# Modulation units over whole k, low one-hot rows on VectorE, chunk loads three ahead, and one gathered prompt row with each batch of the gate table

## The chip, the cores and the metric

The kernel runs on one core of a Trainium2 chip. The metric is the device time of one execution in microseconds. The profile names the engines PE (TensorE matmuls), PEld (its weight loads), DVE (VectorE), ACT (ScalarE), POOL (GpSimd) and SP (SyncE, which here only issues DMA transfers). L997 is line 997 of the kernel before.

## The reference

The kernel computes one inference step of two post-norm layers for 128 prompt tokens and 256 latent tokens of width 1024. Cut to what matters here:

```python
def adaln(cond, w, b):
    m = jax.nn.silu(cond) @ w + b                  # w: 1024 x 6144 in each layer, two vectors cond
    return jnp.split(m[..., None, :], 6, axis=-1)  # shift, scale, gate, twice

def layer(x, l, cond, ctx):
    sh1, sc1, g1, sh2, sc2, g2 = adaln(cond, w_mod[l], b_mod[l])
    y, new_ctx = token_mixer(modulate(x, sh1, sc1), ...)     # projections, three mixers, output product
    x = layer_norm(DN_ALPHA * x + g1 * y, ...)
    f = peer(modulate(x, sh2, sc2), ...)
    return layer_norm(DN_ALPHA * x + g2 * f, ...), new_ctx

def peer(h, wq, keys, u_tab, v_tab):               # 16384 experts, 8 heads x 16 of them for each token
    ...                                            # e: chosen experts, g: their gates
    act = jax.nn.gelu(einsum('td,ted->te', tb, u_tab[eb])) * gb
    return einsum('te,ted->td', act, v_tab[eb])
```

## The kernel before

The stages follow one another in each layer: start or norm, mixer (projections, three branches, output product), routes (queries and the choice of experts), gate table, expert loop, tail.

All weights arrive as tiles of 128 x 1024 f32 (512 KB) in a pool `wst`, tag `w`, with 8 buffers. SP issues these loads in order; a load waits until a buffer is free, and what stands behind it on SP waits too. Projections run block by block: `blocks` loads a block of `w_in`, `split` casts it on ScalarE (`uh`, L222) and subtracts on VectorE or GpSimd (`ul`, L224), and `proj3` multiplies (L368 to L370).

A modulation unit (`adaln_unit`) yields some columns of `w_mod` for both conditioning vectors. It runs 32-row matmuls in four quadrants of the PSUM tile (L259), copies the sum (L261, `modp`), and the next unit's call finishes it. Before, a unit is 256 columns: two loads, eight matmuls with k spread over the quadrants, two selection products (L265) which add the quadrants, and two ScalarE steps with the bias (L268). There are 48 units: 8 at the start, 16 and 8 as fill between the blocks of the two mixers, 4 in each layer ahead of the routes (the rest of the list in layer 1), 10 during the routes of layer 0. A matmul of f32 by f32 shows as two records in the trace.

Prompt tokens take their experts' rows by gather: GpSimd fetches a 128 x 1024 tile of rows (`prow`, L1057 for u, L1068 for v; 256 in a layer), VectorE multiplies and sums it (L1062 or L1073). `slots` decides how many lie behind which instruction.

Latent tokens go through all 128 chunks of 128 experts. `u_load` fetches a chunk of `peer_uT`, `u_product` multiplies it (L1164 for the first 35 chunks in f32, L1167 to L1169 afterwards in three parts). The first 35 products run during routes and gate table. `gate_table` builds for 16 tokens at a time (16 batches in a layer) the dense table of gates: VectorE makes one-hot rows `oa`, `ol` (L997, L999) and `oh` (L1001), ScalarE scales the low rows `ol` token by token (L1004), TensorE multiplies (L1014, L1015, 32 matmuls in a batch), ScalarE copies out (L1018), and SP writes two 512 KB pieces to `gd` in DRAM. With each batch go W_RATE gathered rows. The expert loop then takes for each chunk the u product, the gates `gt` back from `gd` (L1219, 512 KB in four chunks), and the v product (L1243 to L1245); the remaining rows are spread over its chunks at the pace of

```python
w = (c + 2) * 10 - (10 - P_TAIL) * max(0, c + 2 - (128 - LAG))
slots(n_win + -(-(256 - n_win) * w // (10 * (128 - P_END) - (10 - P_TAIL) * (LAG - P_END))), last[0])
```

where n_win is the number of rows done by the end of the gate table, and P_TAIL, P_END and LAG are 5, 6 and 36: 10/1070 of the rows with each chunk, and half of it in the tail, where only v products are left.

Tile pools and a scheduler set the order of the instructions on each engine.

Of the kernel before, what the change touches and what calls it, by code (L numbers as in the profile page):

```python
# [155 lines left out]
def hybrid_step(ctx: ExitStack, tc: tile.TileContext, A, O):  # L156
# [71 lines left out]
    fill_ps, fill_n, first = [None], [0], [0]  # L228


    def cond_prep(sp, ps1):
# [12 lines left out]
        for l in range(DEPTH):
            bm = mk(sp, [48, 128], "bm", bufs=2)
            dma(out=bm, in_=A["b_mod"][l].rearrange("(k p) -> k p", p=128))
            ps = mk(ps1, [128, 512], "pt")
            T.transpose(ps[:, :48], bm, ident[:48, :48])
            V.tensor_copy(bmT[:, l], ps[:, :48])
            for part in (1, 4):  # L250
                V.tensor_scalar(bmT[:, l, part * KD:(part + 1) * KD], bmT[:, l, part * KD:(part + 1) * KD], 1.0, None, op0=ALU.add)
# [1107 lines left out]
```

## Time and profile before

| | us |
|---|---|
| median of three timed runs | 2998.48 |
| lowest and highest | 2995.82, 3007.12 |
| the profiled execution's own time | 3004.09 |
| its span, first to last instruction | 3002.3 |
| TensorE, VectorE, ScalarE, GpSimd busy | 2855.6, 2309.1, 1396.8, 824.8 |
| DMA | 767.09 MB, 256 GB/s over the span |

Busy time is the union of an engine's instructions; TensorE's matmuls overlap and their ends are modelled, so a busy TensorE is not one at its peak. The rows of a later section are read as follows. A row of a table by stretch has the stretch, its length, then for each engine the busy time and the instructions, the granted TensorE clock (1.00 is 2.4 GHz), the DMA's busy share and GB/s. A row of the timeline has start, duration, engine, line, operation, output and inputs, how many were merged, and in brackets the idle time before it with its releaser.

### The profile page before, as it was taken

The numbers are of one execution on the slowest core, as the hardware profiler recorded it, in microseconds if no ns is written. First come the engines' busy times: TensorE is split into PE (matmuls) and PEld (weight loads), VectorE is DVE, ScalarE is ACT, GpSimd is POOL, SyncE is SP. The second block draws the span as 40 slices with busy tenths as digits, with TensorE's granted clock in tenths as the row PEclk, the third lists the DMA queues.
The fourth block names the chain that finished last, engine by engine and source line by source line (L and its number), as shares of the span: only waits on it lengthen the run. The fifth ranks groups of instructions, "written<-read, shape, count | busy, mean of one in ns | idle before, by whom it ended". The sixth has DMA issues, their size and how long they took to land.

```text
span 3002.3 us, 48719 instructions
## 1 busy us (share of the span) xinstructions
PE 2855.6 (95%) x17953; PEld 2479.3 (83%) x17953; DVE 2309.1 (77%) x4888; ACT 1396.8 (47%) x2861; POOL 824.8 (27%) x566
## 2 busy tenths in 40 slices
PE   7999999999889999999969999999987999999996
PEld 5888889877779999998858888898876999999985
DVE  3645654599669999998976466547986999999988
ACT  4544543225754444444445455432178544444443
POOL 1000000002334455554540000000033444555554
PEclk9999999999889999999979999999999999999998
DMA  6454322565999999999934432233569999999994
GB/s 246 151 159 146 95 72 87 182 223 167 316 364 408 391 392 396 393 391 369 379 97 144 127 93 74 85 111 113 156 217 371 418 395 392 394 391 394 393 364 166
DMA packets 299328, 767.09 MB, mean 256 GB/s; under 512 B 42770, under 2 KB 113874, under 8 KB 299090
## 3 DMA queue, kind: packets, MB, share of 16 engines
q1 hardware_dynamic: 225362, 495.51, 46.2%
q0 software_dynamic: 73728, 268.47, 23.5%
q8 instruction: 141, 2.31, 0.3%
q14 instruction: 97, 0.79, 0.1%
HBM read 726.92 MB, written 36.96 MB: 254 GB/s over the span
## 4 chain that ended last, share of the span: by engine, by line
PE 74%; DVE 11%; DMA 6%; ACT 4%; issue 4%; POOL 1%; SPq 0%; POOLq 0%; ACTq 0%; DVEq 0%
PE hp L1167 6%; PE out L1243 6%; PE hp L1169 6%; PE out L1245 6%; PE hp L1168 6%; PE out L1244 6%; PE pp L368 5%; PE pp L369 5%; PE pp L370 5%; PE hp L1164 4%; DMA w<-in_peer_uT 3%; PE pp L947 2%; ACT ol L1004 2%; DVE vl L224 2%; DVE tn L1073 2%
## 5 line engine op out<-in xcount | busy, mean ns | idle before, releaser
L1057 POOL DMA_INDIRECT prow<-in_peer_u,ei x256 | 363.1, 1418 | 763.1 <-DVE prow L1062 523.5
L1068 POOL DMA_INDIRECT prow<-in_peer_v,ei x256 | 382.4, 1494 | 350.1 <-DVE tn L1073 308.6
L222 ACT CAST vh<-w 128x1024 fp32r<-128x1024 f32 x256 | 268.9, 1050 | 367.9 <-issue 285.8
L1167 PE MATMUL hp<-hh,uh 128*128 128x256 f32 x1488 | 434.7, 292 | 0.0
L1169 PE MATMUL hp<-hh,ul 128*128 128x256 f32 x1488 | 417.1, 280 | 0.0
L1168 PE MATMUL hp<-hl,uh 128*128 128x256 f32 x1488 | 416.5, 280 | 0.0
L1245 PE MATMUL out<-vh,al 128*128 128x512 f32 x1024 | 400.0, 393 | 3.6 <-DVE al L1230 3.6
L1244 PE MATMUL out<-vl,ah 128*128 128x512 f32 x1024 | 397.5, 390 | 2.9 <-DVE vl L224 2.9
L1243 PE MATMUL out<-vh,ah 128*128 128x512 f32 x1024 | 392.9, 400 | 1.4 <-ACT ah L1228 1.4
L224 DVE TENSOR_TENSOR vl<-w,vh 128x1024 fp32r<-128x1024 f32 x256 | 315.8, 1234 | 62.7 <-ACT vh L222 44.0
L1073 DVE SCALAR_TENSOR_TENSOR tn<-prow,pact,tn 128x1024 f32<-128x1024 f32 x254 | 325.4, 1281 | 2.7
L1155 ACT CAST uh<-w 128x1024 fp32r<-128x1024 f32 x186 | 195.2, 1050 | 252.6 <-PE hp L1168 240.6
L368 PE MATMUL pp<-hh,uh 128*128 128x384 f32 (+1 forms) x848 | 297.9, 351 | 7.5 <-ACT hh L344 3.8
L1062 DVE SCALAR_TENSOR_TENSOR prow<-prow,tn 128x1024 f32<-128x1024 f32 x256 | 302.4, 1219 | 0.1
L1164 PE MATMUL hp<-hs,w 128*128 128x256 f32 x1120 | 270.1, 398 | 30.0 <-DMA w<-in_peer_uT 30.0
L370 PE MATMUL pp<-hh,ul 128*128 128x384 f32 (+1 forms) x848 | 297.0, 350 | 1.4 <-POOL ul L224 1.4
L369 PE MATMUL pp<-hl,uh 128*128 128x384 f32 (+1 forms) x848 | 294.8, 348 | 0.2 <-DVE xr L494 0.2
L1167 PEld LDWEIGHTS hp<-hh,uh 128*128 128x128 f32 x1488 | 281.1, 189 | 0.0
L1169 PEld LDWEIGHTS hp<-hh,ul 128*128 128x128 f32 x1488 | 281.1, 189 | 0.0
L1168 PEld LDWEIGHTS hp<-hl,uh 128*128 128x128 f32 x1488 | 281.1, 189 | 0.0
L224 DVE TENSOR_TENSOR ul<-w,uh 128x1024 fp32r<-128x1024 f32 x124 | 149.8, 1208 | 162.2 <-ACT uh L222 158.2
L1164 PEld LDWEIGHTS hp<-hs,w 128*128 128x128 f32 x1120 | 218.8, 200 | 63.4 <-DMA w<-in_peer_uT 33.1
(401 smaller groups left out, 5637.9 us busy)
## 6 DMA issues: line engine op xcount, KB each, us to landing
w<-in_peer_uT SPq DMA_DIRECT2D x256, 512.0 KB
w<-in_peer_v SPq DMA_DIRECT2D x256, 512.0 KB
w<-in_w_in SPq DMA_DIRECT2D x104, 512.0 KB
w<-in_w_mod SPq DMA_DIRECT2D x96, 512.0 KB
gd<-w SPq DMA_DIRECT2D x64, 512.0 KB
gt<-gd SPq DMA_DIRECT2D x64, 512.0 KB
w<-in_peer_wq SPq DMA_DIRECT2D x32, 512.0 KB
w<-in_w_branch SPq DMA_DIRECT2D x24, 512.0 KB
```

The lines of the kernel that those rows point to most:

```text
L224: e.tensor_tensor(lo, src, hi.bitcast(F32), op=ALU.subtract)
L368: T.matmul(o, wh[:, k, :], hh[:, k, :], start=(k == 0), stop=False)
L369: T.matmul(o, wh[:, k, :], hl[:, k, :], start=False, stop=False)
L370: T.matmul(o, wl[:, k, :], hh[:, k, :], start=False, stop=(k == KD - 1))
L1073: V.scalar_tensor_tensor(acc, row, act[:, j:j + 1], acc, op0=ALU.mult, op1=ALU.add)
L1164: T.matmul(o, ut[0][:, k, :], hs[:, k, :], start=(k == 0), stop=(k == KD - 1))
L1167: T.matmul(o, uh[:, k, :], hh[:, k, :], start=(k == 0), stop=False)
L1168: T.matmul(o, uh[:, k, :], hl[:, k, :], start=False, stop=False)
L1169: T.matmul(o, ul[:, k, :], hh[:, k, :], start=False, stop=(k == KD - 1))
L1243: T.matmul(o, ah[:, ts], vh[:, ns], start=f, stop=False)
L1244: T.matmul(o, ah[:, ts], vl[:, ns], start=False, stop=False)
L1245: T.matmul(o, al[:, ts], vh[:, ns], start=False, stop=e)
```

## The change

Five things are done. A modulation unit now takes 1024 columns over all eight k: eight loads, 32 matmuls in which each quadrant holds other columns, two transposes in place of the selection products, and additions with the bias on VectorE; there are 12 units (2 at the start, 5 and 2 slots for fill after every sixth block, 1 ahead of the routes, 3 at blocks 9, 12 and 15 of the routes). The conditioning vectors and the bias arrive already transposed. The low one-hot rows are multiplied by one VectorE instruction per batch, with glT in f16. The first three chunks of peer_uT are loaded ahead of the loop and each step loads the chunk three further on. W_RATE is 1 instead of 2.

```diff
-W_RATE = 2
+W_RATE = 1
-N_FILL = (16, 8)
-N_AD = (4, 4)
+N_FILL = (5, 2)
+FILL_BY = 6
+N_AD = (1, 1)
+U_AHEAD = 3
-R_AD = 4
+UNITS = [((0, 0, 0, 4), (0, 1, 0, 4)), ((0, 0, 4, 4), (0, 1, 4, 4))]
+UNITS += [((l, part, 0, 8),) for l, part in ((0, 2), (0, 3), (0, 4), (1, 0), (1, 1), (0, 5), (1, 2), (1, 3), (1, 4), (1, 5))]
...
     def cond_prep(sp, ps1):
-        cond = mk(sp, [16, 128], "cond")
-        dma(out=cond[0:8, :], in_=A["c_ctx"].rearrange("(k p) -> k p", p=128))
-        dma(out=cond[8:16, :], in_=A["c"].rearrange("o (k p) -> (o k) p", p=128))
+        cond = mk(sp, [128, 16], "cond")
+        dma(out=cond, in_=A["cond"])
+        dma(out=bmT, in_=A["b_mod"])
...
-    def adaln_unit(l, part, hb, ps1, tags):
-
-        w = load_k(A["w_mod"][l, part * 4 + hb])
+    def adaln_unit(u, ps1, tags):
+
         ps = mk(ps1, [128, 512], tags[0])
         for k in range(KD):
-            q = k % 4
-            T.matmul(ps[32 * q:32 * q + 32, :256], condT[:, k, :], w[k], start=(k < 4), stop=(k >= 4), tile_position=(0, 32 * q))
+            w = mk(wst, [128, RAWC], "w")
+            dma(out=w, in_=A["w_mod"][u, k])
+            for q in range(4):
+                T.matmul(ps[32 * q:32 * q + 32, :256], condT[:, k, :], w[:, q * 256:(q + 1) * 256], start=(k == 0), stop=(k == KD - 1), tile_position=(0, 32 * q))
         mp = mk(outer, [128, 256], "modp", bufs=2)
         S.copy(mp, ps[:, :256])
         yield
         pt = mk(ps1, [128, 512], tags[1])
         for a in range(2):
-            T.matmul(pt[:, 2 * a:2 * a + 2], mp[:, a * 128:(a + 1) * 128], sel, start=True, stop=True)
-        c = part * KD + 2 * hb
-        for a in range(2):
-            S.activation(mcol[:, l, part, 2 * hb + a, :], pt[:, 2 * a:2 * a + 2], AF.Identity, bias=bmT[:, l, c + a:c + a + 1])
+            T.transpose(pt[:, a * 128:(a + 1) * 128], mp[:, a * 128:(a + 1) * 128], ident)
+
+        pv = pt[:, :256].rearrange("p (a q m) -> p q a m", a=2, q=4)
+        j = 0
+        for l, part, k0, n in UNITS[u]:
+            for c in range(2):
+                V.tensor_tensor(mcol[:, l, part, k0:k0 + n, c].rearrange("p (q a) -> p q a", a=2), pv[:, j // 2:(j + n) // 2, :, c],
+                                bmT[:, l, part * KD + k0:part * KD + k0 + n].rearrange("p (q a) -> p q a", a=2), op=ALU.add)
+            j += n
...
             yield load_w(src[b0 + j])
-            if j % 2 and fill_n[0] > 0:
+            fill_at[0] += 1
+            if fill_n[0] > 0 and fill_at[0] % FILL_BY == 0:
                 fill_n[0] -= 1
                 adaln(1, fill_ps[0], ("pp", "pt"))
...
                 for k in range(KD):
-                    if k % 2 == 0:
-                        adaln(2, ps1, ("pp", "pt"), True)
+                    if k % 4 == 0:
+                        adaln(1, ps1, ("pp", "pt"), True)
...
-        glT = mk(rp, [128, NS], "glT")
+        glT = mk(rp, [128, NS], "glT", dt=F16)
...
-                slot(V.tensor_tensor(oh, ol, bc(ghT), op=ALU.mult))
-                for r in range(TB):
-                    o = ol[:, r // 2, :, r % 2]
-                    S.activation(o, o, AF.Copy, scale=glT[:, b * TB + r:b * TB + r + 1])
+                V.tensor_tensor(oh, ol, bc(ghT), op=ALU.mult)
+                slot(V.tensor_tensor(ol, ol, bc(glT), op=ALU.mult))
...
-        u_load(0)
+        for c in range(U_AHEAD):
+            u_load(c)
 
         def u_step(i):
-            if i + 1 < LAG - 1:
-                u_load(i + 1)
+            if i + U_AHEAD < LAG - 1:
+                u_load(i + U_AHEAD)
             u_product(i)
...
-            if l == 0 and b >= N_WQ + R_AD:
+            if l == 0 and b in (9, 12, 15):
                 adaln(1, pu, ("uT", "hp"), b == 15)
```

On VectorE, in the gate table of layer 0, two batches before stand like this (oa, ol and ohh are one-hot rows, prow a gathered row with its sum hd):

```order
L997 TENSOR_TENSOR oa_7010<-iot_6854,i1T_6850 128x2048
L999 TENSOR_TENSOR ol_7012<-iot_6854,i2T_6851 128x2048
L1001 TENSOR_TENSOR ohh_7014<-ol_7012,ghT_6852 128x2048
L1062 SCALAR_TENSOR_TENSOR prow_7016,hd_6888<-prow_7016,tn_4726 128x1024
L1062 SCALAR_TENSOR_TENSOR prow_7019,hd_6888<-prow_7019,tn_4726 128x1024
L997 TENSOR_TENSOR oa_7095<-iot_6854,i1T_6850 128x2048
```

and at the same place of the change like this:

```order
L1001 TENSOR_TENSOR ol_6893<-iot_6704,i2T_6701 128x2048
L1003 TENSOR_TENSOR ohh_6895<-ol_6893,ghT_6702 128x2048
L999 TENSOR_TENSOR oa_6971<-iot_6704,i1T_6700 128x2048
L1004 TENSOR_TENSOR ol_6893<-ol_6893,glT_6703 128x2048
L1062 SCALAR_TENSOR_TENSOR prow_6898,hd_6739<-prow_6898,tn_4628 128x1024
L1001 TENSOR_TENSOR ol_6973<-iot_6704,i2T_6701 128x2048
```

A batch has five VectorE instructions in both; the multiply by glT has taken the place of one row, and the next batch's oa stands ahead of it.

On SP, in the mixer of layer 0, the loads before alternate between two blocks of w_in and the two tiles of a unit:

```order
L210 DMA w_1050<-in_w_mod 128x1024
L210 DMA w_1052<-in_w_mod 128x1024
L210 DMA w_1480<-in_w_in 128x1024
L210 DMA w_1512<-in_w_in 128x1024
L210 DMA w_1544<-in_w_mod 128x1024
```

and at the same place of the change (the last two blocks ahead of a unit, the unit, the next block):

```order
L214 DMA w_1378<-in_w_in 128x1024
L214 DMA w_1410<-in_w_in 128x1024
L255 DMA w_1443<-in_w_mod 128x1024
L255 DMA w_1449<-in_w_mod 128x1024
L255 DMA w_1455<-in_w_mod 128x1024
L255 DMA w_1461<-in_w_mod 128x1024
L255 DMA w_1467<-in_w_mod 128x1024
L255 DMA w_1473<-in_w_mod 128x1024
L567 DMA out_new_state_ssd<-so_814 128x4x64
L255 DMA w_1479<-in_w_mod 128x1024
L255 DMA w_1485<-in_w_mod 128x1024
L567 DMA out_new_state_ssd<-so_824 128x4x64
```

The next block's load (w_1498) now follows behind these eight.

## Rows read from the trace of the kernel before

**Rows 1.** The page, the chain that ended last, by engine.
```profile
PE 74%; DVE 11%; DMA 6%; ACT 4%; issue 4%; POOL 1%; SPq 0%; POOLq 0%; ACTq 0%; DVEq 0%
```

**Rows 2.** Table by stretch: engines' busy us, granted clock, DMA share, GB/s.
```profile
50.00:525.00 475.00, 468.65 (x2951) 402.22 (x2950) 264.47 (x577) 216.28 (x501) 10.96 (x6) 0.98 0.38 121
717.00:862.00 145.00, 118.67 (x855) 100.69 (x853) 93.01 (x114) 113.59 (x344) 53.03 (x32) 0.90 0.92 301
...
868.00:900.00 32.00, 32.00 (x201) 29.24 (x201) 30.83 (x48) 17.00 (x25) 15.78 (x11) 0.94 1.03 418
...
1142.00:1400.00 258.00, 258.00 (x1690) 233.28 (x1689) 246.96 (x271) 119.86 (x177) 131.77 (x94) 1.00 1.01 393
1411.00:1500.00 89.00, 88.34 (x422) 71.94 (x422) 86.20 (x115) 43.38 (x60) 45.65 (x25) 1.00 0.98 368
...
2196.00:2321.00 125.00, 100.34 (x787) 85.30 (x785) 92.80 (x114) 111.08 (x339) 50.20 (x32) 0.95 0.98 333
2250.00:2275.00 25.00, 20.75 (x155) 17.91 (x156) 20.12 (x24) 23.65 (x75) 10.25 (x7) 0.93 1.08 375
```

**Rows 3.** Chain of the gate-table stages, by line, and two of its pieces.
```profile
by line: DMA w<-in_peer_uT 31.4%; PE hp L1164 28.6%; ACT ol L1004 17.1%; ACT w L1018 6.0%; DMA gd<-w 3.9%; DMA gt<-gd 3.0%; issue 2.6%; PE pn L1015 1.1%; PE pn L1014 0.9%; DVE ohh L1001 0.8%; PE pp L1014 0.8%; PE pp L1015 0.8%; DVE oa L997 
by line: DMA w<-in_peer_uT 28.9%; ACT ol L1004 27.8%; PE hp L1164 14.8%; ACT w L1018 10.5%; DMA gd<-w 4.8%; DMA gt<-gd 3.2%; issue 3.2%; SPq L1021 1.6%; DVE ohh L1001 0.9%; ACT gel L1171 0.9%; DVE oa L997 0.9%; DVE ol L999 0.9%; PE pn L1015
...
746.21 10.01 DMA w<-in_peer_uT
...
760.73 3.52 PE hp L1164 x16
```

**Rows 4.** Line L997 in each layer (first and last start), and its neighbours' timeline.
```profile
L997 DVE TENSOR_TENSOR oa<-iot,i1T x16: 1218/1221/1226, 716.6 to 843.4; 128x2048 f16<-128x2048 f16 x16
L997 DVE TENSOR_TENSOR oa<-iot,i1T x16: 1218/1225/1226, 2194.8 to 2299.6; 128x2048 f16<-128x2048 f16 x16
...
734.31 1.22 DVE L997 TENSOR_TENSOR oa<-iot,i1T 128x2048 f16<-128x2048 f16 x1
769.86 0.22 PE L1014 MATMUL pn<-ohh,oa 128*128 128x128 f16 x1 [0.28 <-ACT w L1018]
771.41 4.82 ACT L1004 ACTIVATE ol<-ol,glT 128x128 f16<-128x128 f16 x16
771.76 3.67 PE L1164 MATMUL hp<-hs,w 128*128 128x256 f32 x16
```

**Rows 5.** Groups by line: busy us, mean ns of one, idle before.
```profile
L1001 DVE TENSOR_TENSOR ohh<-ol,ghT 128x2048 f16<-128x2048 f16 x32 | 39.2, 1224 | 1.0
L1073 DVE SCALAR_TENSOR_TENSOR tn<-prow,pact,tn 128x1024 f32<-128x1024 f32 x254 | 325.4, 1281 | 2.7
L222 ACT CAST uh<-w 128x1024 fp32r<-128x1024 f32 (+1 forms) x130 | 134.6, 1038 | 203.8 <-PE pp L369 162.2 <-issue 24.0 <-PE pb L691 12.4
L224 DVE TENSOR_TENSOR ul<-w,uh 128x1024 fp32r<-128x1024 f32 x124 | 149.8, 1208 | 162.2 <-ACT uh L222 158.2 <-PE pt L412 2.8 <-PE pt L265 0.5
```

**Rows 6.** The start: timeline, a piece of the chain, GB/s from 4 to 50 us.
```profile
4.13 24.35 SPq L210 DMA_DIRECT2D w<-in_w_mod  x16
21.84 1.26 ACT L444 ACTIVATE hraw<-pa,mcol 128x128 f32<-128x128 f32 x3
24.00 0.51 ACT L344 CAST hh<-hraw 128x384 fp32r<-128x384 f32 x1
51.78 0.69 PE L370 MATMUL pp<-hh,ul 128*128 128x384 f32 x1 [1.44 <-POOL ul L224]
...
9.71 3.85 DMA w<-in_w_mod
...
GB/s 394 346 413 389 395 413 417 420 374 417 420 413 424 424 410 417 342 232 256 239 214 196 367 324 256 264 228 214 128 388 356 175 319 24 0 0 6 6 156 381
```

**Rows 7.** Chain during the routes: pieces of one modulation unit.
```profile
599.13 0.56 PE uT L259 x6
599.69 0.54 PE hp L265 x4
```

More of the change, by code (lines that the diff above doesn't have):

```diff
@@ L227, in hybrid_step @@
     spool = [None]
-    fill_ps, fill_n, first = [None], [0], [0]
+    fill_ps, fill_n, fill_at, first = [None], [0], [0], [0]
     def cond_prep(sp, ps1):
-        cond = mk(sp, [16, 128], "cond")
-        dma(out=cond[0:8, :], in_=A["c_ctx"].rearrange("(k p) -> k p", p=128))
-        dma(out=cond[8:16, :], in_=A["c"].rearrange("o (k p) -> (o k) p", p=128))
+        cond = mk(sp, [128, 16], "cond")
+        dma(out=cond, in_=A["cond"])
+        dma(out=bmT, in_=A["b_mod"])
         V.memset(condT, 0.0)
-        ps = mk(ps1, [128, 512], "pt")
-        T.transpose(ps[:, :16], cond, ident[:16, :16])
@@ L238, in cond_prep @@
         th = mk(sp, [128, 16], "cth")
-        S.activation(th, ps[:, :16], AF.Tanh, scale=0.5)
+        S.activation(th, cond, AF.Tanh, scale=0.5)
         cc = mk(sp, [128, 16], "cc")
-        S.activation(cc, ps[:, :16], AF.Copy, scale=0.5)
+        S.activation(cc, cond, AF.Copy, scale=0.5)
         V.scalar_tensor_tensor(condT[:, :, 0:2].rearrange("p k c -> p c k"), th.rearrange("p (c k) -> p c k", c=2), 1.0,
                                cc.rearrange("p (c k) -> p c k", c=2), op0=ALU.add, op1=ALU.mult)
[L244 to L251, printed above, removed]
@@ L253, in adaln_unit @@
-    def adaln_unit(l, part, hb, ps1, tags):
-        w = load_k(A["w_mod"][l, part * 4 + hb])
+        for part in (1, 4):
+            b = bmT[:, :, part * KD:(part + 1) * KD]
+            V.tensor_scalar(b, b, 1.0, None, op0=ALU.add)
+    def adaln_unit(u, ps1, tags):
         ps = mk(ps1, [128, 512], tags[0])
         for k in range(KD):
-            q = k % 4
-            T.matmul(ps[32 * q:32 * q + 32, :256], condT[:, k, :], w[k], start=(k < 4), stop=(k >= 4), tile_position=(0, 32 * q))
+            w = mk(wst, [128, RAWC], "w")
+            dma(out=w, in_=A["w_mod"][u, k])
+            for q in range(4):
+                T.matmul(ps[32 * q:32 * q + 32, :256], condT[:, k, :], w[:, q * 256:(q + 1) * 256], start=(k == 0), stop=(k == KD - 1), tile_position=(0, 32 * q))
@@ L264, in adaln_unit @@
         for a in range(2):
-            T.matmul(pt[:, 2 * a:2 * a + 2], mp[:, a * 128:(a + 1) * 128], sel, start=True, stop=True)
-        c = part * KD + 2 * hb
-        for a in range(2):
-            S.activation(mcol[:, l, part, 2 * hb + a, :], pt[:, 2 * a:2 * a + 2], AF.Identity, bias=bmT[:, l, c + a:c + a + 1])
-    todo = []
-    for l, ps in ((0, (0, 1)), (0, (2,)), (0, (3, 4)), (1, (0, 1)), (0, (5,)), (1, (2,)), (1, (3, 4)), (1, (5,))):
-        todo += [(l, part, hb) for hb in range(4) for part in ps]
+            T.transpose(pt[:, a * 128:(a + 1) * 128], mp[:, a * 128:(a + 1) * 128], ident)
[6 more added lines that the diff above has]
+            j += n
+    todo = list(range(len(UNITS)))
     begun = []
@@ L277, in adaln @@
         for _ in range(min(n, len(todo))):
-            u = adaln_unit(*todo.pop(0), ps1, tags)
+            u = adaln_unit(todo.pop(0), ps1, tags)
             next(u)
@@ L449, in mixer @@
                 ln_mod_T(l, t, 0, 1, sp, mk(sp, [128, D], "xn", bufs=3), ps1, "pt", raw, lambda ks: parts(raw[:, ks], hh[:, ks, ts], hl[:, ks, ts], V if t == 2 else G))
-        fill_ps[0], fill_n[0], first[0] = ps1, N_FILL[l], N_FIRST
+        fill_ps[0], fill_n[0], fill_at[0], first[0] = ps1, N_FILL[l], 0, N_FIRST
         ysT = [mk(mo, [128, 4, NTOK], f"y{i}", dt=F32 if i else F32R) for i in range(3)]
@@ L1329, in blocked @@
     d["peer_wq"] = cut(d["peer_wq"], KD, 128)[:, :, 0]
-    d["w_mod"] = cut(d["w_mod"], 4, 256)
+    m = d["w_mod"].reshape(DEPTH, KD, 128, 6, KD, 128)
+    d["w_mod"] = np.stack([np.concatenate([m[l, :, :, part, k0:k0 + n].reshape(KD, 128, n * 128) for l, part, k0, n in u], axis=2) for u in UNITS])
+    d["b_mod"] = d["b_mod"].reshape(DEPTH, 48, 128).transpose(2, 0, 1)
+    d["cond"] = np.concatenate([d.pop("c_ctx").reshape(KD, 128), d.pop("c").reshape(KD, 128)]).T
     d["w_out"] = cut(d["w_out"], 4, 256)
```

## Prediction

> **What bounds the kernel now.** I read the page first: TensorE holds 74% of the chain that ended last, VectorE 11% and the DMA 6% [rows 1]. One core, so no other core's time matters. Then the table of busy time by stretch [rows 2], because the average hides three different regimes in each of the two layers. In the long expert loop (row 1142 to 1400) TensorE is busy in all of it, VectorE in 246.96 of 258 us (96%) and the DMA moves 393 GB/s. In the loop's tail (1411 to 1500) VectorE is busy 86.20 of 89 us. In the gate-table stage (717 to 862 and 2196 to 2321) nobody is full: TensorE 118.67 of 145 us at a granted clock of 0.90, VectorE 93.01, ScalarE 113.59.
>
> Third, the chain by line in the gate-table stage [rows 3]: the wait for a chunk of `peer_uT` is 31.4% of it in layer 0 and 28.9% in layer 1, ScalarE's `ol` at L1004 17.1% and 27.8%. One such wait is 10.01 us, for a product (16 L1164 matmuls) that takes 3.52 us. So this is a stage of late loads, and I look for the gain there.
>
> **The change, part by part.** The sum is made on the profiled execution's own 3004.1 us; the median of the three timed runs, 2998.5 us, lies 5.6 us below it, and I move the result down by that.
>
> *Gate table, 16 batches a layer.* The 16 ScalarE instructions a batch (4.82 us together, [rows 4]) go; one VectorE multiply of the form of L1001 (1224 ns) comes [rows 5]; one row's product goes from the batch. VectorE so has five operations a batch as before. Unhindered, its first three batches took from 716.6 to 734.31 us, 5.9 us each [rows 4]; that stays its floor. Over all 15 intervals the batches took (843.4-716.6)/15 = 8.45 us in layer 0 and (2299.6-2194.8)/15 = 6.99 in layer 1 [rows 4]. TensorE's floor in layer 0: 21 chunk products over 16 batches, 1.31 x 3.52 us, and 1.9 us for the batch's 32 f16 matmuls (from the first at 769.86 to the next product at 771.76, [rows 4]), 6.5 us; in layer 1 17 products, 1.06 x 3.52 + 1.9 = 5.6 us. DMA: a batch writes 1.05 MB of table, gathers one row of 0.52 MB instead of two, and loads 0.69 or 0.56 MB of chunks: 2.26 and 2.13 MB, at 375 GB/s (best row of this stage, 2250 to 2275 [rows 2]) 6.0 and 5.7 us. The chunks are asked for three products early, some 10 us ahead at 3.5 us each, about the 10.01 us of the longest kind of wait. The likely periods are a little above the highest floor, 6.7 and 6.2 us: 15 x 1.75 = 26 and 15 x 0.8 = 12 us. Behind the last batch those 4.82 us become one VectorE step of 1.2: 3.6 us a layer. Together **-45 us**. Bounds: -60 at the floors; -12 if the chunks come as late as now and only the ScalarE part helps.
>
> *The 16 rows a layer that leave the batches* go to the expert loop: 240 instead of 224 rows, at the pacing of L1274 (224 x 10/1070) 2.24 a chunk instead of 2.09. A chunk has 38 TensorE records, so 1690 records in 258 us are 5.80 us a chunk [rows 2]. VectorE gets 0.15 x 1.28 us (L1073, [rows 5]) = 0.19 us more, 3.3% of the chunk: 96% becomes 99%. It stays just under TensorE, which hides it; if that cover is gone the excess is paid, so I take +3 us for both layers, 0 to 10. DMA: 1.05 MB of u and v, 0.13 of the table, 2.24 x 0.524 of rows: 2.36 MB in 5.80 us, 406 GB/s. The row 868 to 900 shows 418 GB/s with TensorE full, so I take this as hidden. The tail has no such cover: 30 of the rows' products lie there and become 32; two at 1.28 us a layer, **+5 us**.
>
> *Start.* Sixteen `w_mod` loads are issued from 4.13 on [rows 6], before and after. Before, 8 units run in four rounds of load, product, copy, selection, columns; the first block's products stall for `ul` until 51.78. Now two rounds. At about 400 GB/s (first entries of the GB/s row) 8.4 MB behind 2.2 MB of constants and x have landed by some 28 us; copy, transposes and adds are 2 us; the ScalarE steps for two k run from 21.84 to 24.51, 1.33 us each, so four k are 5.3 us and with two casts between them 7.4. First full product near 38 to 40: **-12 us**, range -6 to -14.
>
> *Units elsewhere.* Products and bytes are equal: one new unit is four old. The four selection matmuls of an old unit (0.54 us [rows 7]) become two transposes in a new one: 40 old units outside the start become 10, so at least 30 x 0.54 = 16 us of TensorE leave, nearly all in stretches where it is the chain; I take **-15**. The additions move to VectorE, 28 small ones, under its other work.
>
> *Eight loads in one burst.* This is where the change adds a wait. The pool `w` has 8 buffers and SP issues in order, so the next block's load stands behind the unit's eight and gets a buffer only when TensorE has done the unit's first k. Behind it wait the cast, the subtraction, and TensorE's next product. A load in a quiet stretch took 3.85 us [rows 6], cast and subtraction 1.04 and 1.21 [rows 5]: 6.1 us. Meanwhile TensorE has the rest of the unit: 64 matmuls at 0.56/6 us [rows 7] are 6.0 us, less the first k 5.2. So about 1 us a unit, ten units: **+10 us**, from 0 to 74 (a landing of 10.01 us gives 12.3-4.9 = 7.4 each). By DMA: Bandwidth & Descriptors of the Trainium skill (section Anatomy of one DMA), a transfer costs about 2 us fixed plus its bytes at 436 GB/s, by estimate 3.2 us for such a load; by that the stall would be 0.4 us a unit and the sum 6 us lower. That section was measured on another issue path, and the row is used.
>
> In the routes stage of layer 0 the first three chunk loads now hold 3 of the 8 buffers; its three units are counted above.
>
> **Sum:** -45 +3 +5 -12 -15 +10 = -54. 3004.1-54 = 2950 by the profiled execution, **2945 us** by the median.
>
> **Rivals.** *(a) The chunks stay late.* Three held chunks and four table rows being written nearly fill the 8 buffers, so SP stands at the head of its queue as now. For it: the stage's DMA is already at 0.98 busy in layer 1 [rows 2]. Against: a quarter of the gate stage's bytes other than chunks leave. Then -12 instead of -45: 2978 us.
>
> *(b) The DMA bounds the expert loop.* If 393 GB/s were all it gives, 2.36 MB last 6.0 us, 0.2 more for 93 chunks in each layer: +37 instead of +3, 2979 us. Against it stand the 418 GB/s of 868 to 900; for it, that this lasts only while the loop starts up. SBUF — State Buffer of the Trainium skill (section SBUF: two separate sides) gives some 358 GB/s for HBM to a core; by that a chunk would take an estimated 6.6 us and the kernel would end over 100 us slower. The trace disagrees already before the change: 393 and 418 GB/s.
>
> *(c) The bursts starve TensorE,* the case that ends slower. The sum without stalls is -64; ten units cancel it from 6.4 us a unit, and at the 7.4 us of a late landing the time is 3008 us. Against it: between 50 and 525 the DMA is busy only 0.38 [rows 2], so a landing there should be nearer 3.85 than 10.
>
> *(d) Everything goes to its floor:* gate stage -60, units -20, no stalls, tail +5, start -12: -87, 2912 us.
>
> **Chances.** The forecast 0.59 (its own range 2925 to 2968), (a) 0.14, (b) 0.08, (c) 0.07, (d) 0.12. The range reaches to (d) below and past (a) and (b) above: 2912 to 2982. About 0.5%, 15 us, is what a measurement of this kernel can tell from no change. Faster than 2983: the forecast, (d) and most of (a) and (b), 0.87; the same: the rest of them and the milder half of (c), 0.08; slower 0.05.
>
> **What would show it.** Starts of the batches' first VectorE operation 6 to 7 us apart in both layers and the wait for `peer_uT` nearly gone from the chain; the first full product near 39 us; the expert loop still with TensorE full and 5.8 us a chunk, at about 406 GB/s; the tail 2 to 3 us longer. I am wrong if TensorE shows idle microseconds behind each unit, if the batches still show gaps near 10 us behind a chunk, or if the loop's chunks take 6 us.

## The result and the profile after

| | before | after |
|---|---|---|
| median of four runs, us | 3002.28 | 2923.86 |
| lowest to highest | 2995.82 to 3007.12 | 2920.87 to 2929.14 |
| the profiled execution, its span | 3004.09, 3002.3 | 2929.14, 2927.4 |

The ratio is 0.9742, 95% interval 0.9715 to 0.9769: the change makes the kernel 2.6% faster. The forecast was 2945, its range 2912 to 2982: the measured median lies 21 us below the forecast, inside the range. The likeliest case's own range, 2925 to 2968, is missed by 1 us, on the side of case (d).

To see where the 74.9 us between the two spans come from, I cut both traces at the same instructions: the first full projection product, the first query product of the latent tokens, the first `oa`, the first and the last u product of the expert loop, in each layer.

| stretch, us | before | after | difference | foreseen |
|---|---|---|---|---|
| start | 49.3 | 32.1 | -17.2 | -12 |
| mixer, layer 0 | 512.0 | 507.1 | -4.9 | with the next rows: -15 + 10 |
| routes, layer 0 | 155.3 | 167.9 | +12.6 | |
| gate table, layer 0 | 151.0 | 115.2 | -35.8 | -45 for both layers |
| expert loop, layer 0 | 539.3 | 539.1 | -0.2 | +3 for both |
| tail and norm | 140.6 | 143.1 | +2.5 | +5 for both |
| mixer, layer 1 | 498.9 | 485.1 | -13.8 | |
| routes, layer 1 | 148.4 | 148.4 | 0 | |
| gate table, layer 1 | 131.6 | 109.9 | -21.7 | |
| expert loop, layer 1 | 538.7 | 539.6 | +0.9 | |
| tail, layer 1 | 137.2 | 139.9 | +2.7 | |

Three of the terms are as forecast (loop +0.7 where 3 was written, tails +5.2 where 5, units and bursts -6.1 where -5, the last by luck, as a later section shows); gate table -57.5 and start -17.2 are larger.

The page of the changed kernel, the chain that ended last, by engine:

```profile
PE 74%; DVE 14%; issue 4%; DMA 4%; ACT 1%; POOL 1%; SPq 0%; POOLq 0%; ACTq 0%; DVEq 0%
```

VectorE's share has grown (11 to 14%), those of the DMA (6 to 4%) and of ScalarE (4 to 1%) have shrunk [rows 1]. The table by stretch, with columns as in [rows 2]; the stretches are the routes and the gate table of layer 0, the gate table of layer 1, the second half of the expert loop of layer 0, its tail:

```profile
539.20:707.10 167.90, 157.37 (x947) 130.73 (x947) 135.89 (x848) 25.03 (x54) 4.87 (x5) 0.95 0.48 170
...
707.00:822.00 115.00, 105.05 (x860) 93.55 (x860) 97.25 (x102) 45.08 (x92) 24.65 (x16) 0.97 0.98 316
...
2138.00:2248.00 110.00, 94.10 (x798) 80.15 (x797) 96.00 (x103) 43.11 (x87) 26.16 (x16) 0.94 0.97 314
...
1100.00:1355.00 255.00, 255.00 (x1668) 230.44 (x1667) 250.03 (x280) 120.53 (x176) 142.51 (x99) 1.00 1.02 406
...
1366.00:1448.00 82.00, 78.89 (x373) 63.94 (x372) 79.76 (x105) 38.88 (x54) 42.55 (x27) 1.00 0.99 375
```

In the gate table of layer 0 TensorE is now busy in 105 of 115 us at a clock of 0.97 (before 118.67 of 145 at 0.90 [rows 2]), and ScalarE has gone from 113.59 to 45.08. The expert loop has 1668 records in 255 us, 38 of them a chunk, so 5.81 us a chunk at 406 GB/s with TensorE full: what the forecast said. The routes are now 167.9 us long, and TensorE is busy in 157.37 of them. The same stretch of the kernel before:

```profile
561.30:716.60 155.30, 155.28 (x949) 128.46 (x948) 134.09 (x842) 31.58 (x81) 4.87 (x5) 1.00 0.48 164
```

There 155.28 of 155.3 us were busy, at a clock of 1.00 instead of 0.95: ten idle microseconds are new.

The chain in the gate tables of the changed kernel, layer 0 and layer 1, by line:

```profile
by line: PE hp L1164 42.5%; DVE ohh L1003 6.2%; DVE ol L1004 6.0%; DVE oa L999 6.0%; DVE ol L1001 6.0%; DVE prow L1062 5.0%; DMA gd<-w 4.6%; PE pn L1015 4.5%; PE pn L1014 4.3%; PE pp L1015 4.2%; PE pp L1014 4.2%; DMA gt<-gd 3.6%; issue 1.1%
...
by line: PE hp L1164 18.5%; DVE ohh L1003 9.5%; DVE ol L1001 9.3%; DMA gd<-w 8.5%; DVE ol L1004 8.4%; DVE oa L999 8.3%; DVE prow L1062 8.3%; DMA w<-in_peer_uT 6.7%; DMA gt<-gd 3.9%; PE pn L1014 3.1%; SPq L1021 3.0%; PE pn L1015 3.0%; PE pp 
```

The wait for `peer_uT`, 31.4 and 28.9% before [rows 3], is out of the first and 6.7% of the second. Layer 0 now follows TensorE (products and the four L1014/L1015 groups, some 60%), layer 1 VectorE. The `oa` of the batches, first and last start in each layer, against [rows 4]:

```profile
L999 DVE TENSOR_TENSOR oa<-iot,i1T x16: 1215/1218/1225, 707.1 to 797.7; 128x2048 f16<-128x2048 f16 x16
...
L999 DVE TENSOR_TENSOR oa<-iot,i1T x16: 1212/1216/1226, 2138.0 to 2222.2; 128x2048 f16<-128x2048 f16 x16
```

The periods are (797.7-707.1)/15 = 6.04 and (2222.2-2138.0)/15 = 5.61 us, where 6.7 and 6.2 were written. Both lie below the floors that the prediction had worked out (6.5 for TensorE in layer 0, 5.9 for VectorE in layer 1). The stretches from the first to the last `oa`, columns as above:

```profile
707.10:797.70 90.60, 89.97 (x741) 80.00 (x740) 87.59 (x92) 36.37 (x77) 22.03 (x14) 1.00 0.96 311
...
2138.00:2222.20 84.20, 82.05 (x692) 69.41 (x692) 82.94 (x90) 34.25 (x73) 23.51 (x14) 1.00 0.95 309
```

In layer 0 TensorE is busy in 89.97 of 90.6 us, in layer 1 VectorE in 82.94 of 84.2: these stretches are full.

Where the late chunks came from shows on SP. The longest wait of its queue (waiting line, what it waited for, us in total, times, longest); the first row is of the kernel before (717 to 862), the second of the change (707 to 817):

```profile
SPq L1021 <- ACT w L1018: 95.5, 31, 20.6
```

```profile
SPq L1021 <- ACT w L1018: 28.3, 13, 11.9
```

SP stood 95.5 of 145 us at a table write whose data ScalarE had not yet copied out, and every chunk load behind that write stood too. The chain of [rows 3] names only the DMA, but the load stood behind a wait for ScalarE's copies. In the change this wait is 28.3 of 110 us. Which edit took it away is for the experiments: one puts the low rows back on ScalarE, one takes the look-ahead away, one takes the writes off SP.

The ten idle microseconds of the routes are in the units. A piece of the chain, one of the three (start, us, what):

```profile
585.77 0.98 PE uT L257 x10
586.75 0.86 PE pn L923 x6
587.62 1.03 PE uT L257 x15
...
588.66 4.90 DMA w<-in_w_mod
...
593.61 0.75 PE uT L257 x8
...
594.80 0.70 PE hp L263 x2
```

The first four k go through at 0.64 us each; then the product waits for each of the last four loads. In that time SP issued `w_mod` in two parts, four loads early and four from 585.80 on, as the products of the first k gave their buffers back: three of the eight buffers held chunks of `peer_uT`, whose first product (L1164) starts at 656.4, 70 us later.

The six units in the two mixers leave smaller waits. Behind one of them, the chain in the mixer of layer 0, and the product's idle time from the timeline:

```profile
168.38 3.44 DMA w<-in_w_in
...
171.84 1.05 ACT uh L226
...
172.91 1.24 DVE ul L228
...
172.93 0.44 PE L369 MATMUL pp<-hh,uh 128*128 128x384 f32 x1 [0.81 <-ACT uh L226]
```

The next block's load is issued when the unit's first products give a buffer back, and its cast and its subtraction come after TensorE has finished the unit. Behind four of the six units TensorE so waits 0.9 to 1.5 us, 4.5 us together, and behind the unit ahead of the routes 2.6 us for the query weights (0.8 before). The kernel before has such a wait only at its start.

The start, ScalarE and TensorE (columns as in [rows 4]):

```profile
20.17 0.37 ACT L259 COPY modp<-pp 128x256 f32<-128x256 f32 x1 [5.55 <-PE pp L257]
21.41 1.26 ACT L446 ACTIVATE hraw<-pa,mcol 128x128 f32<-128x128 f32 x3 [0.86 <-DVE mcol L269]
...
26.15 0.51 ACT L345 CAST hh<-hraw 128x384 fp32r<-128x384 f32 x1
...
30.48 0.37 ACT L259 COPY modp<-pp 128x256 f32<-128x256 f32 x1 [3.82 <-PE pp L257]
...
32.07 0.69 PE L369 MATMUL pp<-hh,uh 128*128 128x384 f32 x1 [0.47 <-ACT uh L226]
```

The columns of the first unit are used from 21.41 on, and ScalarE's work for its four k ends at 26.66, while the second unit's loads still land; the first product runs at 32.07.

### The profile page after: what moved, and what is told of

Its sections match the earlier page's. It is cut to its first block, busy times and chain, and to the rows that moved or that the text cites. A ratio compares the mean times of both kernels' runs of the same rounds, so it can differ in the third digit from the quotient of the medians.

```text
span 2927.4 us, 47722 instructions
## 1 busy us (share of the span) xinstructions
PE 2799.1 (96%) x17782; PEld 2443.5 (83%) x17782; DVE 2346.7 (80%) x4944; ACT 1234.2 (42%) x2217; POOL 815.7 (28%) x566
## 4 chain that ended last, share of the span: by engine, by line
PE 74%; DVE 14%; issue 4%; DMA 4%; ACT 1%; POOL 1%; SPq 0%; POOLq 0%; ACTq 0%; DVEq 0%
PE hp L1167 6%; PE out L1244 6%; PE out L1246 6%; PE hp L1169 6%; PE hp L1168 6%; PE out L1245 6%; PE pp L371 4%; PE pp L369 4%; PE pp L370 4%; PE hp L1164 4%; PE pp L949 2%; DVE vl L228 2%; PE hp L1225 1%; PE pp L859 1%; PE pp L917 1%
## 5 line engine op out<-in xcount | busy, mean ns | idle before, releaser
L1068 POOL DMA_INDIRECT prow<-in_peer_v,ei x256 | 376.4, 1470 | 310.7 <-DVE tn L1073 278.1
L228 DVE TENSOR_TENSOR vl<-w,vh 128x1024 fp32r<-128x1024 f32 x256 | 316.0, 1234 | 41.0 <-ACT vh L226 39.8
L352 POOL TENSOR_TENSOR res<-res,lg 128x384 f32<-128x384 f32 x6 | 8.8, 1465 | 895.3 <-ACT res L314 895.3
L1164 PE MATMUL hp<-hs,w 128*128 128x256 f32 x1120 | 255.7, 383 | 1.5 <-DMA w<-in_peer_uT 1.5
## 6 DMA issues: line engine op xcount, KB each, us to landing
w<-in_peer_uT SPq DMA_DIRECT2D x256, 512.0 KB, 7.8
w<-in_peer_v SPq DMA_DIRECT2D x256, 512.0 KB, 8.1
w<-in_w_in SPq DMA_DIRECT2D x104, 512.0 KB, 4.3
w<-in_w_mod SPq DMA_DIRECT2D x96, 512.0 KB, 4.7
gd<-w SPq DMA_DIRECT2D x64, 512.0 KB, 7.7
gt<-gd SPq DMA_DIRECT2D x64, 512.0 KB, 8.0
w<-in_peer_wq SPq DMA_DIRECT2D x32, 512.0 KB, 3.8
w<-in_w_branch SPq DMA_DIRECT2D x24, 512.0 KB, 3.5
```

The lines of the kernel that those rows point to most:

```text
L228: e.tensor_tensor(lo, src, hi.bitcast(F32), op=ALU.subtract)
L1068: G.indirect_dma_start(out=row, out_offset=None, in_=vtab, in_offset=bass.IndirectOffsetOnAxis(ap=ei[:, j:j + 1], axis=0))
L1164: T.matmul(o, ut[0][:, k, :], hs[:, k, :], start=(k == 0), stop=(k == KD - 1))
```

## The experiments

Twelve kernels ran, each beside the kernel before on the same chip. Theory A and rival B concern the routes of layer 0; the other theories concern the gate table or the tail.

**The units alone.** The changed kernel with the three gate-table edits undone:

```diff
-W_RATE = 1
+W_RATE = 2
-U_AHEAD = 3
+U_AHEAD = 1
...
-        glT = mk(rp, [128, NS], "glT", dt=F16)
+        glT = mk(rp, [128, NS], "glT")
...
-                V.tensor_tensor(oh, ol, bc(ghT), op=ALU.mult)
-                slot(V.tensor_tensor(ol, ol, bc(glT), op=ALU.mult))
+                slot(V.tensor_tensor(oh, ol, bc(ghT), op=ALU.mult))
+                for r in range(TB):
+                    ...
+                    S.activation(o, o, AF.Copy, scale=glT[:, b * TB + r:b * TB + r + 1])
```

> The new modulation units alone, with the gate table, the low one-hot rows on ScalarE, two rows a batch and chunks asked one ahead as in the kernel before. Theory A, that the three chunk tiles held through the routes of layer 0 leave the units' eight loads too few buffers: here only one is held, so the three units in those routes lose about 1 us instead of 10, the start gains 17, the two mixers 19, together 32 us less than before, 2968 us. Rival B, that eight loads in one burst are late there whatever is held: the routes keep the 10 us of stalls, 23 us less than before, 2977 us. Both expect the gate-table stages unchanged, 151 and 132 us.

Measured 2968.07 us, ratio 0.9895 (0.9879 to 0.9912). The routes of layer 0 take 155.1 us, as before the change (155.3), with the same three units in them; the start -17.1, the mixers -14.6, the gate tables take 149.4 and 130.8. That is theory A, with 30 us gained where it had 32.

**The gate-table edits alone**, the same lines the other way, in the kernel before.

> The gate-table edits alone (low rows by one VectorE multiply, chunks three ahead, one row a batch) on the old modulation units. Both theories expect the gate-table stages at about 115 and 110 us, 57 us less together, the tails 5 us longer, 52 us less than before, 2948 us. By theory A the gains of this run and of the run with the units alone add to more than the change gave (32 + 52 against 75 us), because the held chunk tiles cost nothing where a unit asks for two tiles at a time: the routes of layer 0 stay at 157 us. By rival B they add to the 75.

Measured 2953.55 us, ratio 0.9856 (0.9836 to 0.9876). The routes stay at 155.3 us with three chunks held: old units ask for two tiles at a time. The gate tables take 114.1 and 116.6, the tails are 5.2 longer. In layer 1 that is 6.7 longer than in the change, and the cause is not settled (a chunk load of 9.55 us, issued behind four table writes, stands in its chain). That the two gains add to more than the change gave can't be read from the medians (29.8 and 44.3 in this comparison, 74.1, against 78.4 of the change in its own): their spread is too large. By the spans of the profiled executions, one of each kernel, it is 33.4 + 50.1 = 83.5 against 74.9.

**The low rows back on ScalarE**, in the changed kernel (the last two hunks of the first experiment, `glT` and the multiply, alone).

> The change with the low one-hot rows multiplied on ScalarE again, 16 instructions a batch. If the batches now stand at the pace of the slowest engine, that becomes ScalarE with some 7.2 us a batch (115.69 us busy in 16 batches before) instead of VectorE's 5.8: the two stages about 15 us longer each, 2950 us or a little above. Rival: the late chunks were all that mattered, the multiply's place is worth nothing, and the time stays within 8 us of 2924.

Measured 2952.95 us, ratio 0.9846 (0.9829 to 0.9862): the gate tables take 125.6 and 123.5 us instead of 115.2 and 109.9. SP stands at its writes for 74.9 of 120 us in layer 0, but TensorE waits only 4.0 us for chunks there (13.6 in the kernel before): asked for three ahead, they are in time. The chain in layer 1 shows whose pace it is:

```profile
by line: ACT ol L1006 41.8%; ACT w L1020 18.2%; PE hp L1166 10.2%; DMA w<-in_peer_uT 7.2%; issue 3.9%; DMA gt<-gd 3.5%; DMA gd<-w 3.3%; ACT gel L1173 2.4%; PE pn L1016 1.6%; PE pp L1017 1.5%; PE pp L1016 1.4%; PE pn L1017 1.4%; DVE ohh L100
```

**Chunks one ahead**, in the changed kernel:

```diff
-U_AHEAD = 3
+U_AHEAD = 1
```

> The change with chunks of peer_uT asked one product ahead, not three. If the look-ahead is what took the late chunks away, the wait for them returns, and the gate-table stages grow by about 20 and 12 us, while the routes of layer 0 get back some 9 us by theory A: about 2947 us. Rival: the fewer gathered bytes took the late chunks away by themselves; then the stages stay at 115 and 110 us, and the time falls to 2915 us by theory A or stays at 2924 by rival B.

Measured 2933.74 us, ratio 0.9792 (0.9775 to 0.9808). The routes are back at 155.0 (theory A), the gate tables take 127.7 and 116.3, so 12.5 and 6.4 longer, not 20 and 12: the mechanism is right, its size too large. The chain in layer 0, a piece of it, and SP's longest wait there (691 to 814):

```profile
by line: PE hp L1164 33.1%; DMA w<-in_peer_uT 26.0%; ACT w L1018 7.2%; DMA gt<-gd 3.2%; DMA gd<-w 3.0%; PE pn L1015 3.0%; PE pn L1014 2.8%; DVE ol L1004 2.7%; DVE oa L999 2.7%; DVE ohh L1003 2.7%; DVE ol L1001 2.7%; SPq L1021 2.0%; PE pp L1
...
777.62 2.08 ACT w L1018 x4
...
780.12 8.93 DMA w<-in_peer_uT
...
789.10 3.72 PE hp L1164 x16
...
SPq L1021 <- ACT w L1018: 83.8, 31, 18.8
```

SP stands at the writes as long as before, 83.8 of 123 us, though ScalarE has no low rows any more and mostly waits for TensorE itself (67.5 us at L1171). So the low rows on ScalarE are not what held the writes here. The piece shows a ring: the copies of a batch wait for its products, the write for the copies, the next chunk's load for the write, the chunk's product for the load, and the next batch's products stand behind that product on TensorE. The look-ahead opens the ring.

**Two rows a batch**, in the changed kernel:

```diff
-W_RATE = 1
+W_RATE = 2
```

> The change with two gathered rows a batch again instead of one. If VectorE is what a batch now waits for (five operations, 5.8 us), a sixth makes it 7.0 us: 16 x 1.2 = 19 us more in each gate-table stage, and the tails give back 2.5 us each: about 2957 us. Rival: VectorE has room in the batch, since chunk loads were the limit, and the stages grow by less than 8 us each: below 2938 us.

Measured 2967.32 us, ratio 0.9885 (0.9852 to 0.9917). Gate tables 136.8 and 133.6, so 21.6 and 23.7 longer; tails 2.5 shorter each. The chain in layer 0 and its stretch:

```profile
by line: DMA w<-in_peer_uT 25.2%; PE hp L1164 14.0%; DVE prow L1062 11.7%; DMA gd<-w 7.7%; DVE oa L999 6.8%; DVE ol L1004 6.8%; DVE ohh L1003 6.7%; DVE ol L1001 6.6%; DMA gt<-gd 3.0%; PE pn L1015 2.5%; PE pn L1014 2.1%; PE pp L1015 2.1%; PE
```

```profile
707.00:844.00 137.00, 111.71 (x862) 96.00 (x861) 114.06 (x135) 45.08 (x91) 54.28 (x32) 0.91 0.97 328
```

The late chunks are back, at 25.2%, and VectorE has 114 of 137 us. So the size fits VectorE and the chain fits the bytes; the next run was to tell them apart.

**One VectorE instruction done twice**, in the changed kernel:

```diff
-                V.tensor_tensor(oh, ol, bc(ghT), op=ALU.mult)
+                for _ in range(2):
+                    V.tensor_tensor(oh, ol, bc(ghT), op=ALU.mult)
```

> The change with one VectorE instruction of each batch (the multiply of the high rows) done twice, which alters no value: a sixth VectorE operation of 1.22 us a batch as with two rows a batch, but without the second row's 0.52 MB. Theory VectorE: the second row cost the gate tables 22 and 24 us by its place on VectorE, and this run loses as much, some 18 us a stage, about 2961 us. Theory bytes: the second row's gather delayed the chunk loads, whose wait came back into the chain; then VectorE's sixth operation alone costs the first layer little (TensorE is busy 105 of 115 us there), the second some 10 us: about 2938 us.

Measured 2983.05 us, ratio 0.9932 (0.9916 to 0.9947): 59 us lost, more than either theory. Layer 0 loses 19.8, the size that VectorE's time would have, though the chunk loads are 17.1% of its chain too; layer 1 loses 39.8, with less for the DMA to do than in the run before. Its chain, its stretch, SP's waits and a piece of SP's queue in layer 1:

```profile
by line: DMA w<-in_peer_uT 25.2%; PE hp L1165 16.3%; DVE ohh L1004 6.9%; ACT w L1019 6.4%; DMA gd<-w 5.9%; PE pn L1016 5.5%; PE pn L1015 4.5%; PE pp L1016 4.2%; DVE oa L999 3.8%; PE pp L1015 3.8%; DVE ol L1001 3.1%; issue 3.1%; DMA gt<-gd 2
```

```profile
2158.00:2308.00 150.00, 105.98 (x796) 90.27 (x797) 114.34 (x119) 44.09 (x87) 26.15 (x16) 0.86 0.75 229
```

```profile
SPq L1022 <- ACT w L1019: 110.8, 27, 15.6
```

```profile
2202.81 5.97 SPq L1022 DMA_DIRECT2D gd<-w  x4
2208.88 1.24 SPq L1149 DMA_DIRECT2D w<-in_peer_uT  x2
```

The same queue in the change:

```profile
2186.28 2.77 SPq L1021 DMA_DIRECT2D gd<-w  x2
2190.57 2.47 SPq L1148 DMA_DIRECT2D w<-in_peer_uT  x1
```

Chunks are late (25.2%) with the DMA at 0.75 of its time. With the doubled instruction the queue has another order: four table writes stand on SP ahead of two chunk loads, where the change mostly has two writes and one load. SP waits 110.8 us at writes, against 39.1 in the change. So this run doesn't tell VectorE's time from bytes. It shows something else: the chunks come late here while bandwidth is free, and they stand on SP behind more writes.

**The writes off SP**, in the kernel before:

```diff
-                        dma(out=gd[t0:t0 + 8]...
+                        nc.scalar.dma_start(out=gd[t0:t0 + 8]...
```

> The kernel before, with one edit: the writes of the gate table to DRAM are issued by ScalarE, which makes their data, so that on SP no chunk load stands behind a write that waits for ScalarE. Theory queue: the late chunks of before are loads that stand on SP behind such writes (SP waited 95 of 145 us for ScalarE's copies in layer 0, 28 of 110 after the change). Then the wait for peer_uT goes from 31% of the chain to under 10%, and the stages fall to ScalarE's pace, as where only the low rows went back to it: 126 and 124 us, 2965 to 2970 us. Rival: the loads are late for bytes (two gathered rows a batch) or because they are asked for only one product ahead; the stages stay at 145 us or more and 128 or more, 2990 us or above; ScalarE, which also has to issue 32 writes, may even lose.

Measured 3001.24 us, ratio 0.9995 (0.9980 to 1.0010), no change. The chain in layer 0 and in layer 1:

```profile
by line: ACT ol L1004 43.0%; ACT w L1018 13.7%; PE hp L1164 7.0%; DMA gd<-w 6.3%; DMA w<-in_peer_uT 5.3%; issue 3.9%; ACTq L1021 3.6%; DMA gt<-gd 2.7%; ACT gel L1171 2.6%; PE pn L1014 1.3%; PE pp L1014 1.2%; PE hp L1167 1.0%; PE pn L1015 0.
...
by line: ACT ol L1004 53.2%; ACT w L1018 15.7%; issue 7.5%; DMA gd<-w 4.8%; ACT gel L1171 4.0%; DMA gt<-gd 3.1%; PE hp L1164 2.7%; ACTq L1021 2.6%; PE pn L1014 1.3%; PE pn L1015 1.0%; PE hp L1224 0.9%; PE pp L1014 0.8%; PE pp L1015 0.8%; PE
```

Half of the theory held: the wait for `peer_uT` fell from 31.4 and 28.9% [rows 3] to 5.3 and 2.7%. The gain did not come: ScalarE took the wait's place at once (`ol`, 17.1 and 27.8% before, 43.0 and 53.2% now), in stages of 143.5 and 136.0 us instead of 151.0 and 131.6, not the 126 and 124 expected. SP's loads were not free either: they waited 103.8 of 150 us in layer 0 for buffers which the table writes gave back. Little came of that, since TensorE waited 2.9 us for chunks. By Trainium Kernel Development and Optimization of the Trainium skill (section Key Constraints), issuing from several engines saves only the issue time, since all queues run on the same DMA engines. The time agrees here; the waits don't, since what a transfer stands behind on its queue changed too.

**One chunk held**, in the changed kernel:

```diff
-        for c in range(U_AHEAD):
-            u_load(c)
+        u_load(0)
         def u_step(i):
+            for c in range(1, U_AHEAD) if i == 0 else ():
+                u_load(c)
```

> The change with only the first chunk loaded ahead of the routes; the second and third are asked for with the first product, behind the last unit, and from there on the order of the loads is that of the change. Theory A (held tiles starve the units): the stalls in the routes of layer 0 fall from some 10 us to 1 or 2 and the stage from 170 to about 161 us; the gate tables stay; 2915 us. Rival B (eight loads in a burst are late whatever is held): the stage stays at 170 us, 2924 us.

Measured 2908.63 us, ratio 0.9698 (0.9676 to 0.9720), 15 us better than the change. The routes take 155.1 us instead of 167.9, the gate tables 113.9 and 108.1. TensorE's waits in the routes, of the change and of this run:

```profile
PE uT L257 <- DMA w<-in_w_mod: 9.0, 12, 1.6
```

```profile
PE uT L257 <- DMA w<-in_w_mod: 2.0, 2, 1.5
```

Twelve waits have become two. Theory A is shown for the routes: it is the held tiles, not the burst. The stretch, with columns as above:

```profile
538.60:693.70 155.10, 150.03 (x947) 127.46 (x946) 135.33 (x848) 24.98 (x54) 4.86 (x5) 0.99 0.52 184
```

Of the 12.8 us only 5.4 are idle time (10.5 in the change, 5.1 here). The other 7.3 are busy time: the same 947 records took 157.37 us, in runs broken by the waits and at a granted clock of 0.95, and take 150.03 at 0.99.

**No rows in the gate table**, with one chunk held (the run before), and

```diff
-W_RATE = 1
+W_RATE = 0
```

> One chunk held through the routes, as in the run before, and no gathered row in the gate table at all; all 256 rows of a layer in the expert loop and its tail. If the gate tables now stand near TensorE's floor (105 of 114 us busy in layer 0, 94 of 108 in layer 1), they get only some 5 and 8 us shorter, the tails 2.5 us longer each, and the loop, where VectorE then has 539 us of work in 538, some 5 to 8 us longer each: 2908 to 2920 us, no gain. Rival: each row that leaves gives what the step from two to one gave, 20 us a stage, and the loop still hides the rows: 2880 us.

Measured 2917.21 us, ratio 0.9719 (0.9704 to 0.9734), 9 us worse than with one row. Gate tables 113.0 and 99.7, so nothing and 8.4 gained; loops 2.1 and 2.6 longer, tails 4.4 and 6.2. In layer 0 the chain is 65% chunk products and next to nothing is gained, so TensorE is the limit there, not VectorE.

**The routes' units in the mixer of layer 1**, in the changed kernel:

```diff
-N_FILL = (5, 2)
+N_FILL = (5, 4)
-            if l == 0 and b in (9, 12, 15):
-                adaln(1, pu, ("uT", "hp"), b == 15)
```

> The change with the three units of the routes of layer 0 moved into the mixer of layer 1, between its blocks. If TensorE has no free time in the routes, they become 3 x 6.2 + 10 = 29 us shorter and the mixer 18 us longer: 2913 us. Rival: without units the routes stand at the pace of VectorE's choice of experts, as in layer 1 (150.3 us), so only 19 us leave there against 18 that come: 2923 us, no change.

Measured 2924.56 us, ratio 0.9748 (0.9722 to 0.9773): no change, as the rival said. In the profiled execution (2912.6 us, the lowest of the four, so its stages are on the short side) the routes take 147.1 us, 20.8 less, with TensorE busy in 134.8 of them (VectorE's choice sets the pace), the mixer 12.0 more. In the routes a unit is partly hidden.

**Fewer rows in the tail**, in the changed kernel:

```diff
-P_TAIL = 5
+P_TAIL = 4
```

> The change with P_TAIL 4 instead of 5: of the 240 rows of a layer behind the gate table, 28 instead of 34 lie in the tail. If TensorE hides VectorE's rows in the expert loop (VectorE 521 of 539 us there, 6 rows more make it 529) and the tail shows every row, each tail gets 6 x 1.28 = 7.7 us shorter and the loop stays at 539 us: 15 us less, 2909 us. Rival: the loop is already at VectorE's or the DMA's limit in its last third, and gets longer by as much as the tail gets shorter: 2924 us.

Measured 2920.19 us, ratio 0.9734 (0.9712 to 0.9755). The medians are 3.7 us apart, which is within the spread of the two kernels, so the stages have to show it: the loop stays at 538.3 and 538.6 us, and the tails give 4.4 and 3.4, half of what six rows cost. The chain in the tail of layer 0, of the change and of this run:

```profile
by line: DVE vl L228 28.9%; issue 21.4%; DVE tn L1073 19.4%; DVE at L1227 10.4%; DVE al L1231 9.6%; PE uT L292 3.4%; PE out L1246 2.2%; PE out L1244 2.2%; PE out L1245 2.1%; ACT vh L226 1.2%; PE hp L1225 0.3%; ACTq L226 0.0%
```

```profile
by line: PE out L1245 30.3%; PE out L1244 30.0%; PE out L1246 30.0%; PE hp L1225 7.3%; DMA gt<-gd 4.8%; PE uT L292 2.5%; issue 0.0%
```

After three or so rows the tail has passed from VectorE to TensorE.

**The two that helped, together**: the hunk of one chunk held, and P_TAIL 4.

> The two edits that helped by themselves, together: one chunk held through the routes, and P_TAIL 4. The places don't touch each other, so the gains should add: the routes at 155 us, the tails 4 us shorter each: 2901 to 2904 us. If the loop, with its 6 more rows a layer, loses what the tail gives, 2908 us.

Measured 2902.74 us, ratio 0.9675 (0.9661 to 0.9688). The routes take 155.1 us, the tails 140.2 and 135.5 (143.1 and 139.9 in the change): the gains add. It is the best version of the study, 21 us below the change by the medians of two comparisons.

## Why the prediction was right, step by step

**Gate table (-45, measured -57.5).** The place was right, and the step that failed is the size of the periods, 6.7 and 6.2 us, taken a little above the highest floor: they measured 6.04 and 5.61, below the floors of 6.5 and 5.9 themselves. The engines named were the right ones, since TensorE in layer 0 and VectorE in layer 1 have next to no room left between the first and the last `oa`; but the floors had too much work in a period. For layer 0 the prediction spread all 16 batches and 21 products over the periods; 14 batches' matmuls and 18 products (290 records of L1164) ran in the 15 periods, and the rest behind the last `oa`; in layer 1 VectorE ran 14 of the 16 batches' rows and multiplies in them. Its bound "-60 at the floors" doesn't follow from its floors either: periods down to 6.5 and 5.9 and 3.6 us a layer are 15 x 1.95 + 15 x 1.09 + 7.2 = 53 us, and the measured 57.5 lies past that. The 3.6 us a layer that were to go behind the last batch did not: from the last `oa` to the expert loop it was 24.2 us before and is 24.6 after in layer 0, 26.8 and 25.7 in layer 1. No part does it alone. Undone one at a time, the low rows cost 24.0 us in both layers, the look-ahead 18.9, the second row 45.3, together 88 of a gain of 57.5: each brings back a bound of its own (ScalarE, chunks, chunks and VectorE), which the other two cannot lift. Moving the writes off SP in the kernel before teaches the same from the other side. Not settled: how much of the second row's 45 us is its time on VectorE and how much its bytes.

**Rival (a), chunks stay late.** It fell. SP did stand at the head of its queue, but at writes whose data were not there, and hardly for buffers (2.7 us at L1148 in 717 to 862). The low rows off ScalarE don't free SP by themselves (83.8 of 123 us with the chunks one ahead); with the chunks three ahead much of the wait stays (74.9 of 120 us with the low rows on ScalarE) but does little harm. The buffers are the next limit in line, as the 103.8 us with the writes off SP show.

**Rows into the loop (+3) and tail (+5).** +0.7 and +5.2. VectorE has 521 of 539 us in the loop, still under TensorE; rival (b) fell too, at 408 GB/s over a whole loop. By HBM Reference of the Trainium skill (section Specifications (TRN2)), the 358 GB/s that were weighed for it are a core's share, and a core streaming alone measures well above it, about 425; with that the trace agrees.

**Start (-12, measured -17.2).** The step put ScalarE's work for the first four k, 7.4 us, behind the last load. The two units are cut by k, so the first unit's four k were modulated while the second unit's loads landed, and the first product starts 1.6 us after the second unit's copy (30.48).

**Units and bursts (-15 and +10, measured -6.1 together).** The sum came out by luck. Over the two mixers and the routes of layer 0 TensorE's busy time fell by 20.7 us (1147.3 to 1126.6) and its idle time grew by 14.6 (18.9 to 33.5): both terms were larger, and the differences cancel. The picture behind the +10 (1 us at each of ten units, for the next block's load behind the burst) held outside the routes: some 6 us at seven units, though it was worked out with 6.0 us for a unit's 64 records where a run without waits takes 3.66. What failed is the sentence that counts the three units of the routes with the others. The prediction saw three buffers held there and put no price on it, and the wait came in the middle of the unit, for its own loads. That cost 12.8 us by the run with one chunk held, 4.3 us a unit: of rival (c) the mechanism was real, with 4.3 us instead of 7.4 and at three units instead of ten. With one chunk held the busy time falls by 30.7 and the idle time grows by 8.7, close to the 10 written.

## What to carry to other kernels

When the chain names a load, ask the issuing queue what it stood behind: here a "late DMA" was a load behind a table write that waited for its data on the same in-order queue, and a load asked for early enough took no harm from it. A stage with several engines near their limits gives up its time only when all of the bounds leave; undo the parts one by one, and expect the losses to add to more than the gain. A look-ahead is paid for in buffers over all the time that they are held: ask for the first tiles just ahead of the use, not ahead of another stage that lives from the same pool.

## What the hardware showed that was not expected

Late data cost TensorE twice. A piece of TensorE's timeline in the kernel before, and the table by stretch around it:

```profile
737.51 0.22 PE L1014 MATMUL pn<-ohh,oa 128*128 128x128 f16 x1 [3.31 <-ACT w L1018]
...
740.23 4.70 PE L1164 MATMUL hp<-hs,w 128*128 128x256 f32 x16 [0.17 <-DMA w<-in_peer_uT]
```

```profile
735.00:746.00 11.00, 8.31 (x70) 7.28 (x70) 10.93 (x14) 11.00 (x34) 6.67 (x5) 0.84 1.07 374
```

TensorE stood 3.31 us, the clock granted in this stretch is 0.84, and the chunk product behind it took 4.70 us where another took 3.67 [rows 4]. Over the gate table of layer 0 the groups of chunk products are, before and after (busy us, mean ns of one, idle before):

```profile
L1164 PE MATMUL hp<-hs,w 128*128 128x256 f32 x333 | 88.0, 419 | 13.6 <-DMA w<-in_peer_uT 13.6
```

```profile
L1164 PE MATMUL hp<-hs,w 128*128 128x256 f32 x334 | 76.4, 382 | 0.0
```

The same products cost 11.6 us less where TensorE no longer stops, about a third of the 35.8 us that the stage gained (granted clock 0.90 before [rows 2], 0.97 after; 1.00 is 2.4 GHz, and 1.2 GHz the other level). The prediction used 3.52 us for a product in its floor and measured periods for the kernel before, so this part of the gain was in its difference without a name. The routes of the change pay in the same way: 7.3 of their 12.8 us are busy time, at a granted clock of 0.95 instead of 0.99.
